# Sliding windows by DMA alone: the last staged batch shifted by one block, so that every store takes 128 partitions and the fixes are arranged anew

## The chip, the cores and the metric

One core of a Trainium2 chip. SP, ACT and POOL are engines of the core; here they compute nothing and only issue DMAs, each into a queue of its own, and 16 DMA engines carry the packets of all queues. A semaphore counts what a DMA has finished, by small "semaphore packets"; a DMA has landed when its count is full. The metric is the device time of one execution in microseconds, the median over several runs.

## The reference

```python
batch, length, dim = (32, 4096, 256)       # float32
window_size, stride = 64, 32
n_windows = (length - window_size) // stride + 1        # 127
for i in range(n_windows):
    result[:, i] = x[:, i*stride : i*stride + window_size].copy()
```

Nothing is computed. A block is 32 rows of 256 floats, 32 KB. A batch has 128 blocks. Window w of a batch is its blocks w and w+1, 64 KB, so that nearly every block is written twice. The output has 266.3 MB.

## The kernel before

There are two ways to make a batch, and the kernel mixes them.

- **Direct** (21 batches, SP's queue): a DMA copies 16 windows from DRAM to DRAM. A DMA of whole windows gives each of the 16 DMA engines two packets of 32 KB and one semaphore packet. A "split turn" makes the same copy as two DMAs of half windows: two data packets and two semaphore packets. Splitting slows this queue a little against the others; that is the purpose.
- **Staged** (11 batches, ACT's queue): the batch is loaded once, one block in each of 128 partitions, and stored twice, once as first halves and once as second halves of windows. 128 partitions make 128 half windows, but a batch has 127 windows, so each store also writes one half window of a neighbouring batch with wrong data (the "spill"). Of the direct neighbours some 15 windows are therefore left out and copied at the end, from POOL's queue, after the spilling stores have landed (the "fixes").

The last staged batch, number 30, does not spill. It is stored in four parts, and nothing waits for it but the end of the program:

```python
        if g == len(self.batches) - 1:
            for half, p0, rows in ((0, 0, 112), (0, 112, 15), (1, 1, 15), (1, 16, 112)):
                self.c.count_last(self.c.store(q, self.tiles[i], self.batches[g], half, p0, rows))
            return
        for half in (0, 1):
            self.c.store(q, self.tiles[i], self.batches[g], half).then_inc(self.stored[i], 16)
...
    staged = [*range(1, B - 3, 3), B - 2]
    direct = [b for b in range(B) if b not in staged]
...
                share += 9 if at < loads else 3
                if share >= 12:
                    share -= 12
                    turns += 4
                    c.windows(ring_d, b, first(b) + 16 * j, 16, 0)        # a split turn
                    c.windows(ring_d, b, first(b) + 16 * j, 16, 1, count=mark if todo == 3 else None)
                else:
                    turns += 3
                    c.windows(ring_d, b, first(b) + 16 * j, 16, count=mark if todo == 3 else None)
...
        ring_r.wait_ge(near, 16)          # the last direct DMA but two has landed
        for i, b in enumerate(sorted(rests, key=lambda b: max(waits[b], default=0))):
            for g in waits[b]:
                st.wait_stored(ring_r, g)
            for w, n in rest_parts(b):
                c.windows(ring_r, b, w, n, None, PIECES[i % 1], count_soft)     # 15 windows
```

Of the kernel before, what the change touches and what calls it, by code (L numbers as in the profile page):

```python
# [6 lines left out]


DIRECT, IN, OUT = 32768, 16384, 16384
PIECES = (32768,)  # L10


class Copier:


    def __init__(self, nc, tc, x, out, B, L, D, W, S, n_win):
        assert W == 2 * S and L % S == 0
        self.nc, self.tc, self.x, self.out = nc, tc, x, out
        self.B = B
        self.blk = S * D  # L20
        self.nb = L // S
        self.nw = n_win
        self.total = 0
        self.done = tc.alloc_semaphore("done")
        self.last = tc.alloc_semaphore("last")
        self.last_total = 0

    def xap(self, block, dims):
        return bass.AP(self.x.tensor, self.x.offset + block * self.blk, dims)

    def oap(self, elem, dims):
        return bass.AP(self.out.tensor, self.out.offset + elem, dims)

    def count(self, dma):
        dma.then_inc(self.done, 16)
        self.total += 16

    def count_last(self, dma):
        dma.then_inc(self.last, 16)
        self.last_total += 16  # L40

    def windows(self, q, b, w0, n, half=None, piece=DIRECT, count=None):

        blk = self.blk
        size = 2 * blk if half is None else blk
        off = blk if half else 0
        (count or self.count)(
            q.dma_start(  # L48
                out=self.oap((b * self.nw + w0) * 2 * blk + off, [[2 * blk, n], [1, size]]),
                in_=bass.AP(  # L50
                    self.x.tensor,
                    self.x.offset + (b * self.nb + w0) * blk + off,
                    [[blk, n], [1, size]],
                ),
                max_dma_last_dim=piece,
            )
        )

    def load(self, q, t, b):
        return q.dma_start(  # L60
            out=t[:, :], in_=self.xap(b * self.nb, [[self.blk, self.nb], [1, self.blk]]),
            max_dma_last_dim=IN,
        )

    def store(self, q, t, b, half, p0=0, n=None):



        blk = self.blk
        n = self.nb if n is None else n  # L70
        w = b * self.nw + p0 - half
        return q.dma_start(
            out=self.oap(w * 2 * blk + half * blk, [[2 * blk, n], [1, blk]]),
            in_=t[p0 : p0 + n, :],
            max_dma_last_dim=OUT,
        )


class Staging:


    def __init__(self, c, pool, dtype, batches, bufs):
        self.c, self.batches = c, batches
        self.tiles = [pool.tile([128, c.blk], dtype, name=f"xb{i}") for i in range(bufs)]
        self.loaded = [c.tc.alloc_semaphore(f"loaded{i}") for i in range(bufs)]
        self.stored = [c.tc.alloc_semaphore(f"stored{i}") for i in range(bufs)]

    def load(self, q, g):
        n, i = divmod(g, len(self.tiles))
        if n:  # L90
            q.wait_ge(self.stored[i], 32 * n)
        self.c.load(q, self.tiles[i], self.batches[g]).then_inc(self.loaded[i], 16)

    def store(self, q, g):
        n, i = divmod(g, len(self.tiles))
        q.wait_ge(self.loaded[i], 16 * (n + 1))
        if g == len(self.batches) - 1:

            for half, p0, rows in ((0, 0, 112), (0, 112, 15), (1, 1, 15), (1, 16, 112)):
                self.c.count_last(self.c.store(q, self.tiles[i], self.batches[g], half, p0, rows))  # L100
            return
        for half in (0, 1):
            self.c.store(q, self.tiles[i], self.batches[g], half).then_inc(self.stored[i], 16)

    def wait_stored(self, q, g):
        n, i = divmod(g, len(self.tiles))
# [12 lines left out]
@with_exitstack  # L119
def kernel(  # L120
    ctx: ExitStack,
    tc: tile.TileContext,
    x: bass.AP,
    window_size: bass.AP,
    stride: bass.AP,
    out: bass.AP,
):
    nc = tc.nc
    W, S = int(window_size), int(stride)
    B, L, D = x.shape  # L130
    n_win = (L - W) // S + 1
    assert out.shape == (B, n_win, W, D)
    c = Copier(nc, tc, x, out, B, L, D, W, S, n_win)
    staged = [*range(1, B - 3, 3), B - 2]
    direct = [b for b in range(B) if b not in staged]
    pool = ctx.enter_context(tc.tile_pool(name="xb", bufs=1))
    st = Staging(c, pool, x.dtype, staged, 6)
    ring_d, ring_s = nc.sync, nc.scalar
    spilled = staged[:-1]

    waits = {b: [g for g, n in enumerate(spilled) if abs(n - b) == 1] for b in direct}
    per, loads, stores = 6, 6 * 17, 34

    def first(b):
        return 0 if b - 1 not in spilled else 8 if len(waits[b]) == 2 else 15

    def rest_parts(b):
        if len(waits[b]) == 2:
            return [(0, 8), (120, 7)]
        return [(0 if b - 1 in spilled else 112, 15)]  # L150

    soft = tc.alloc_semaphore("soft")
    soft_total = 0

    near = tc.alloc_semaphore("near")

    def mark(dma):
        dma.then_inc(near, 16)

    def count_soft(dma):  # L160
        nonlocal soft_total
        dma.then_inc(soft, 16)
        soft_total += 16

    with tc.tile_critical():  # L165
        st.run(ring_s)

        turns = share = 0
        rests = []
        todo = 7 * len(direct)  # L170
        for b in direct:
            for j in range(7):
                at = turns % (loads + per * stores)
                share += 9 if at < loads else 3
                if share >= 12:
                    share -= 12
                    turns += 4
                    c.windows(ring_d, b, first(b) + 16 * j, 16, 0)
                    c.windows(ring_d, b, first(b) + 16 * j, 16, 1, count=mark if todo == 3 else None)
                else:  # L180
                    turns += 3
                    c.windows(ring_d, b, first(b) + 16 * j, 16, count=mark if todo == 3 else None)
                todo -= 1
            rests.append(b)

        ring_r = nc.gpsimd
        ring_r.wait_ge(near, 16)
        for i, b in enumerate(sorted(rests, key=lambda b: max(waits[b], default=0))):
            for g in waits[b]:
                st.wait_stored(ring_r, g)  # L190
            for w, n in rest_parts(b):
                c.windows(ring_r, b, w, n, None, PIECES[i % 1], count_soft)
        ring_d.wait_ge(c.done, c.total)
        ring_d.wait_ge(soft, soft_total)
        ring_d.wait_ge(c.last, c.last_total)


# [33 lines left out]
```

## Time and profile before

| what | before |
|---|---|
| time, median (three runs at first; six with those beside the changed kernel) | 752.06 us; 752.27 us |
| profiled execution | 745.32 us, span 743.5 us |
| moved by DMA | 313.16 MB at 421 GB/s |
| ACT's last store data ends (DMA records) | 732.7 us |
| POOL's last fix data ends (DMA records) | 740.1 us |

The page of the kernel before, first the DMA slices (40 equal parts of the span: busy tenths, then GB/s), then the queues (q1 is SP's, q10 ACT's, q0 POOL's: packets, MB, share of 16 engines' time):

```profile
DMA  8999999999999999999999999999999999999995
GB/s 368 431 430 427 426 436 436 423 440 420 431 432 425 427 438 420 435 427 421 439 423 408 431 434 432 434 424 433 427 437 429 430 425 437 421 435 432 414 420 191
q1 hardware_dynamic: 8080, 154.15, 48.5%
q10 hardware_dynamic: 9002, 138.35, 43.8%
q0 software_dynamic: 1008, 20.65, 6.8%
```

The engines are full from the second slice to the last but one. No engine that computes is in sight. Only the bytes, the rate and the two ends can change the time. The waits of POOL in the kernel before (us in total, times, longest):

```profile
POOL out_dram L48 <- DMA out_dram<-in_x_dram: 651.4, 1, 651.4
POOL out_dram L48 <- DMA out_dram<-xb: 22.9, 1, 22.9
```

POOL waits until SP's queue is nearly through, issues 19 fixes, waits 22.9 us for the last spilling stores and issues the other two at 685.8 us. From there to the end nothing waits for anything but bytes: two queues drain.

### The profile page before, as it was taken

The numbers are of one execution on the slowest core, as the hardware profiler recorded it, in microseconds if no ns is written. First come the engines' busy times: TensorE is split into PE (matmuls) and PEld (weight loads), VectorE is DVE, ScalarE is ACT, GpSimd is POOL, SyncE is SP. The second block draws the span as 40 slices with busy tenths as digits, with TensorE's granted clock in tenths as the row PEclk, the third lists the DMA queues.
The fourth block names the chain that finished last, engine by engine and source line by source line (L and its number), as shares of the span: only waits on it lengthen the run. The fifth ranks groups of instructions, "written<-read, shape, count | busy, mean of one in ns | idle before, by whom it ended". The sixth has DMA issues, their size and how long they took to land.

```text
span 743.5 us, 321 instructions
## 1 busy us (share of the span) xinstructions
POOL 12.4 (2%) x25
## 2 busy tenths in 40 slices
POOL 0000000000000000000000000000000000050000
DMA  8999999999999999999999999999999999999995
GB/s 368 431 430 427 426 436 436 423 440 420 431 432 425 427 438 420 435 427 421 439 423 408 431 434 432 434 424 433 427 437 429 430 425 437 421 435 432 414 420 191
DMA packets 18092, 313.16 MB, mean 421 GB/s; under 512 B 4312, under 2 KB 4312, under 8 KB 4312
## 3 DMA queue, kind: packets, MB, share of 16 engines
q1 hardware_dynamic: 8080, 154.15, 48.5%
q10 hardware_dynamic: 9002, 138.35, 43.8%
q0 software_dynamic: 1008, 20.65, 6.8%
q14 instruction: 2, 0.02, 0.0%
HBM read 220.92 MB, written 266.99 MB: 656 GB/s over the span
## 4 chain that ended last, share of the span: by engine, by line
another core or an unknown queue 91%; POOL 2%; issue 0%; POOLq 0%; SPq 0%
POOL out_dram L48 2%; POOLq L226 0%; SPq L165 0%; POOLq L107 0%
## 5 line engine op out<-in xcount | busy, mean ns | idle before, releaser
L48 POOL DMA_DIRECT2D out_dram<-in_x_dram x21 | 12.2, 584 | 674.3 <-DMA out_dram<-in_x_dram 651.4
L212 POOL MEMSET const-float32-0.0<- 128x1 f32 x1 | 0.1, 93 | 0.2 <-issue 0.2
L212 POOL MEMSET const-bfloat16-1.0<- 128x1 bf16 x1 | 0.1, 97 | 0.0
L212 POOL MEMSET const-uint8-127<- 128x1 uint8 x1 | 0.1, 93 | 0.0
L212 POOL MEMSET const-float32-1.0<- 128x1 f32 x1 | 0.1, 92 | 0.0
## 6 DMA issues: line engine op xcount, KB each, us to landing
out_dram<-in_x_dram SPq DMA_DIRECT2D x83, 1024.0 KB, 97.1
out_dram<-xb ACTq DMA_DIRECT2D x20, 4096.0 KB, 137.8
out_dram<-in_x_dram SPq DMA_DIRECT2D x128, 512.0 KB, 90.5
xb<-in_x_dram ACTq DMA_DIRECT2D x11, 4096.0 KB, 122.1
out_dram<-in_x_dram POOLq DMA_DIRECT2D x21, 960.0 KB, 46.5
out_dram<-xb ACTq DMA_DIRECT2D x2, 3584.0 KB, 127.3
out_dram<-xb ACTq DMA_DIRECT2D x2, 480.0 KB, 112.8
```

The lines of the kernel that those rows point to most:

```text
L48: q.dma_start(out=self.oap((b * self.nw + w0) * 2 * blk + off, [[2 * blk, n], [1, size]]), in_=bass.AP(self.x.tensor, self.x.offset + (b * ...
L212: nc = _bacc.Bacc("TRN2", target_bir_lowering=False, num_devices=1)
```

## The change

The last staged batch becomes number 31, and its load starts one block early: partition 0 holds the last block of batch 30, partitions 1 to 127 hold blocks 0 to 126 of batch 31. Both stores take 128 partitions (an even share for all engines), and what they spill falls into windows 125 and 126 of batch 30 alone. Those two windows are patched by a last DMA of 128 KB, after the very last store. The missing last half window of batch 31 is a DMA of 32 KB on SP's queue. Besides, the share of split turns in the store phase falls from 3/12 to 1/12.

```diff
-    staged = [*range(1, B - 3, 3), B - 2]
+    staged = [*range(1, B, 3)]
@@ load and store
-            out=t[:, :], in_=self.xap(b * self.nb, [[self.blk, self.nb], [1, self.blk]]),
+            out=t[:, :],
+            in_=self.xap(b * self.nb - shift, [[self.blk, self.nb], [1, self.blk]]),
@@ Staging.store
-        if g == len(self.batches) - 1:
-            for half, p0, rows in ((0, 0, 112), (0, 112, 15), (1, 1, 15), (1, 16, 112)):
-                self.c.count_last(...)
-            return
         for half in (0, 1):
-            self.c.store(q, self.tiles[i], self.batches[g], half).then_inc(self.stored[i], 16)
+            self.c.store(q, self.tiles[i], self.batches[g], half, self.shift(g)).then_inc(self.stored[i], 16)
@@ direct turns
-                share += 9 if at < loads else 3
+                share += 9 if turns % (loads + per * stores) < loads else 1
...
+                if todo == 7:
+                    count(c.windows(ring_d, B - 1, c.nw - 1, 1, 1, 2048), done)
@@ fixes
+            w, n = (112, 13) if b == last else (0, 15) if b - 1 in staged else (112, 15)
...
+        st.wait_stored(ring_r, len(staged) - 1)
+        ap = [[c.blk // 4, 8], [c.blk, 2], [1, c.blk // 4]]
+        oap = [[c.blk // 4, 8], [2 * c.blk, 2], [1, c.blk // 4]]
+        count(
+            ring_r.dma_start(
+                out=c.oap((last * c.nw + c.nw - 2) * 2, oap), in_=c.xap(last * c.nb + c.nw - 2, ap)
+            ),
+            rest,
+        )
```

More of the change, by code (lines that the diff above doesn't have):

```diff
@@ L9, with __init__ @@
 DIRECT, IN, OUT = 32768, 16384, 16384
-PIECES = (32768,)
 class Copier:
-    def __init__(self, nc, tc, x, out, B, L, D, W, S, n_win):
+    def __init__(self, x, out, B, L, D, W, S, n_win):
         assert W == 2 * S and L % S == 0
-        self.nc, self.tc, self.x, self.out = nc, tc, x, out
+        self.x, self.out = x, out
         self.B = B
@@ L22, in __init__ @@
         self.nw = n_win
-        self.total = 0
-        self.done = tc.alloc_semaphore("done")
-        self.last = tc.alloc_semaphore("last")
-        self.last_total = 0
     def xap(self, block, dims):
         return bass.AP(self.x.tensor, self.x.offset + block * self.blk, dims)
-    def oap(self, elem, dims):
-        return bass.AP(self.out.tensor, self.out.offset + elem, dims)
-    def count(self, dma):
-        dma.then_inc(self.done, 16)
-        self.total += 16
-    def count_last(self, dma):
-        dma.then_inc(self.last, 16)
-        self.last_total += 16
@@ L42, in windows, with oap @@
-    def windows(self, q, b, w0, n, half=None, piece=DIRECT, count=None):
-        blk = self.blk
-        size = 2 * blk if half is None else blk
-        off = blk if half else 0
-        (count or self.count)(
-            q.dma_start(
-                out=self.oap((b * self.nw + w0) * 2 * blk + off, [[2 * blk, n], [1, size]]),
-                in_=bass.AP(
-                    self.x.tensor,
-                    self.x.offset + (b * self.nb + w0) * blk + off,
-                    [[blk, n], [1, size]],
-                ),
-                max_dma_last_dim=piece,
-            )
+    def oap(self, half_window, dims):
+        return bass.AP(self.out.tensor, self.out.offset + half_window * self.blk, dims)
@@ L57, in windows, with load @@
+    def windows(self, q, b, w0, n, half=None, piece=DIRECT):
+        blk = self.blk
+        row = [1, 2 * blk if half is None else blk]
+        h = half or 0
+        return q.dma_start(
+            out=self.oap((b * self.nw + w0) * 2 + h, [[2 * blk, n], row]),
+            in_=self.xap(b * self.nb + w0 + h, [[blk, n], row]),
+            max_dma_last_dim=piece,
         )
-    def load(self, q, t, b):
+    def load(self, q, t, b, shift):
         return q.dma_start(
-            out=t[:, :], in_=self.xap(b * self.nb, [[self.blk, self.nb], [1, self.blk]]),
+            out=t[:, :],
+            in_=self.xap(b * self.nb - shift, [[self.blk, self.nb], [1, self.blk]]),
@@ L62, in load, with store @@
             max_dma_last_dim=IN,
         )
-    def store(self, q, t, b, half, p0=0, n=None):
-        blk = self.blk
-        n = self.nb if n is None else n
-        w = b * self.nw + p0 - half
+    def store(self, q, t, b, half, shift):
+        w = b * self.nw - half - shift
         return q.dma_start(
-            out=self.oap(w * 2 * blk + half * blk, [[2 * blk, n], [1, blk]]),
-            in_=t[p0 : p0 + n, :],
+            out=self.oap(2 * w + half, [[2 * self.blk, self.nb], [1, self.blk]]),
+            in_=t[:, :],
@@ L79, with __init__, shift @@
 class Staging:
-    def __init__(self, c, pool, dtype, batches, bufs):
-        self.c, self.batches = c, batches
+    def __init__(self, c, tc, pool, dtype, batches, bufs, shifted):
+        self.c, self.batches, self.shifted = c, batches, shifted
         self.tiles = [pool.tile([128, c.blk], dtype, name=f"xb{i}") for i in range(bufs)]
-        self.loaded = [c.tc.alloc_semaphore(f"loaded{i}") for i in range(bufs)]
-        self.stored = [c.tc.alloc_semaphore(f"stored{i}") for i in range(bufs)]
+        self.loaded = [tc.alloc_semaphore(f"loaded{i}") for i in range(bufs)]
+        self.stored = [tc.alloc_semaphore(f"stored{i}") for i in range(bufs)]
+    def shift(self, g):
+        return 1 if self.batches[g] in self.shifted else 0
     def load(self, q, g):
@@ L91, in load @@
             q.wait_ge(self.stored[i], 32 * n)
-        self.c.load(q, self.tiles[i], self.batches[g]).then_inc(self.loaded[i], 16)
+        self.c.load(q, self.tiles[i], self.batches[g], self.shift(g)).then_inc(self.loaded[i], 16)
     def store(self, q, g):
@@ L96, in store @@
         q.wait_ge(self.loaded[i], 16 * (n + 1))
-        if g == len(self.batches) - 1:
-            for half, p0, rows in ((0, 0, 112), (0, 112, 15), (1, 1, 15), (1, 16, 112)):
-                self.c.count_last(self.c.store(q, self.tiles[i], self.batches[g], half, p0, rows))
-            return
         for half in (0, 1):
-            self.c.store(q, self.tiles[i], self.batches[g], half).then_inc(self.stored[i], 16)
+            self.c.store(q, self.tiles[i], self.batches[g], half, self.shift(g)).then_inc(self.stored[i], 16)
     def wait_stored(self, q, g):
@@ L132, with count @@
     assert out.shape == (B, n_win, W, D)
-    c = Copier(nc, tc, x, out, B, L, D, W, S, n_win)
-    staged = [*range(1, B - 3, 3), B - 2]
+    c = Copier(x, out, B, L, D, W, S, n_win)
+    staged = [*range(1, B, 3)]
     direct = [b for b in range(B) if b not in staged]
     pool = ctx.enter_context(tc.tile_pool(name="xb", bufs=1))
-    st = Staging(c, pool, x.dtype, staged, 6)
-    ring_d, ring_s = nc.sync, nc.scalar
-    spilled = staged[:-1]
-    waits = {b: [g for g, n in enumerate(spilled) if abs(n - b) == 1] for b in direct}
-    per, loads, stores = 6, 6 * 17, 34
-    def first(b):
-        return 0 if b - 1 not in spilled else 8 if len(waits[b]) == 2 else 15
-    def rest_parts(b):
-        if len(waits[b]) == 2:
-            return [(0, 8), (120, 7)]
-        return [(0 if b - 1 in spilled else 112, 15)]
-    soft = tc.alloc_semaphore("soft")
-    soft_total = 0
-    near = tc.alloc_semaphore("near")
-    def mark(dma):
-        dma.then_inc(near, 16)
-    def count_soft(dma):
-        nonlocal soft_total
-        dma.then_inc(soft, 16)
-        soft_total += 16
+    st = Staging(c, tc, pool, x.dtype, staged, 6, {B - 1})
+    ring_d, ring_s, ring_r = nc.sync, nc.scalar, nc.gpsimd
+    done = tc.alloc_semaphore("done")
+    near = tc.alloc_semaphore("near")
+    rest = tc.alloc_semaphore("rest")
+    total = {done: 0, near: 0, rest: 0}
+    def count(dma, sem):
+        dma.then_inc(sem, 16)
+        total[sem] += 16
+    per, loads, stores = 6, 6 * 17, 34
+    todo = 7 * len(direct)
+    turns = share = 0
     with tc.tile_critical():
         st.run(ring_s)
-        turns = share = 0
-        rests = []
-        todo = 7 * len(direct)
         for b in direct:
+            w = 15 if b - 1 in staged else 0
             for j in range(7):
-                at = turns % (loads + per * stores)
-                share += 9 if at < loads else 3
+                todo -= 1
+                sem = near if todo == 2 else done
+                share += 9 if turns % (loads + per * stores) < loads else 1
                 if share >= 12:
@@ L177 @@
                     turns += 4
-                    c.windows(ring_d, b, first(b) + 16 * j, 16, 0)
-                    c.windows(ring_d, b, first(b) + 16 * j, 16, 1, count=mark if todo == 3 else None)
+                    count(c.windows(ring_d, b, w, 16, 0), done)
+                    count(c.windows(ring_d, b, w, 16, 1), sem)
                 else:
                     turns += 3
-                    c.windows(ring_d, b, first(b) + 16 * j, 16, count=mark if todo == 3 else None)
-                todo -= 1
-            rests.append(b)
-        ring_r = nc.gpsimd
+                    count(c.windows(ring_d, b, w, 16), sem)
+                w += 16
+                if todo == 7:
+                    count(c.windows(ring_d, B - 1, c.nw - 1, 1, 1, 2048), done)
         ring_r.wait_ge(near, 16)
-        for i, b in enumerate(sorted(rests, key=lambda b: max(waits[b], default=0))):
-            for g in waits[b]:
-                st.wait_stored(ring_r, g)
-            for w, n in rest_parts(b):
-                c.windows(ring_r, b, w, n, None, PIECES[i % 1], count_soft)
-        ring_d.wait_ge(c.done, c.total)
-        ring_d.wait_ge(soft, soft_total)
-        ring_d.wait_ge(c.last, c.last_total)
+        pieces = (32768,)
+        last = B - 2
+        for i, b in enumerate([*direct[:-1], last]):
+            for g, n in enumerate(staged):
+                if abs(n - b) == 1 and b != last:
+                    st.wait_stored(ring_r, g)
+            w, n = (112, 13) if b == last else (0, 15) if b - 1 in staged else (112, 15)
+            count(c.windows(ring_r, b, w, n, None, pieces[i % len(pieces)]), rest)
+        st.wait_stored(ring_r, len(staged) - 1)
[7 more added lines that the diff above has]
+        )
+        for sem in (done, near, rest):
+            ring_d.wait_ge(sem, total[sem])
 _INS = ['x', 'window_size', 'stride']
```

## The prediction

> **What bounds it now.** Not a compute engine: the program is all DMA. The page's slices show the 16 DMA engines at 90% or more from slice 2 to slice 39, 313.16 MB at a mean 421 GB/s. In the trace's DMA records a 32 KB packet takes 1.213 us (median), a 16 KB packet 0.611, a semaphore packet 0.009: packet size costs almost nothing, and 16 engines give at most about 430 GB/s; the stretches from 50 to 700 us read 419 to 439. The Trainium skill (DMA: Bandwidth & Descriptors, Where 436 GB/s comes from) puts the ceiling of the ports at 435 GB/s; this trace agrees. Only the bytes and the two ends of the span can move the time.
>
> **Bytes.** 11 staged and 21 direct batches in both kernels. The last staged batch stores 256 half windows instead of 254; POOL's fixes shrink from 315 windows to 313 plus one 128 KB patch; one 32 KB piece is new: under 0.1 MB in all, about 0.2 us. SP issues 196 DMAs instead of 211 (15 x 0.009 us, nothing). Two 15-row stores that left an engine 2.4 us less loaded (4 x 0.611) become full.
>
> **Split of the engines.** The engines seem to take turns by packet between queues. In the store phase SP's queue moves about 241 GB/s, ACT's about 187. Fewer split turns give SP 64 KB in about 3.08 turns instead of 3.25: its queue ends, and POOL's fixes start, about 8 us earlier by my turn count, and ACT's stores end that much later. The sum stays.
>
> **The tail.** Before (span clock, DMA records): ACT's stores end at 726 to 728 us on most engines, 734.0 on the slowest; POOL's fixes, which don't depend on the last stores, end at 735 to 736.5 and 740.1 on the slowest; the span ends 3.4 us after. After: the fixes and ACT's last store end about together, 735 to 736 us, slowest 739 to 740. Then comes a new serial chain: the shifted batch spills into batch 30, so the 128 KB patch may be issued only when the very last store has landed on every engine. From landing to first packet on POOL's queue took 4.8 us before (SP landing at 651.6, POOL issue of 0.6, first packet at 656.3); 8 KB packets then take about 0.6 us, their landing 0.5. That is 5 to 6 us of idle engines, all on the critical path, against at most 1 us gained by the more even last store.
>
> **Prediction.** 752.06 + 5.5 - 1 = about 756.5 us, +0.6%. Range 751 to 761. Chances: faster by over 2% 0.01, within 2% 0.95, slower by over 2% 0.04.
>
> **What would show it.** The rate between 50 and 700 us stays at 425 to 435 GB/s. SP's queue ends near 653 us instead of 661.4. POOL's wait before the fixes shortens to about 643 us; a new wait of POOL for an xb store appears at about 740 us, with one POOL DMA after it, and the chain of waits ends in it.
>
> **What would make it wrong.** If ACT's last store lands several us before POOL's fixes end, the patch hides behind them: equal, or 1 to 3 us better. If ACT's stores drag alone at the end, the loss is still the patch. If POOL's latency on an idle queue is nearer 2 us (4.8 was under load), the loss is 2 to 3 us. If HBM reads and writes clash more when SP has more of the engines, the rate falls everywhere.

## More of the kernel before

All runs told of here were at a granted clock of 1.0. The times come in two levels, whatever the kernel: in some calls the kernel before takes about 746 us, in others about 752 us. All kernels of one call run on the same chip beside the kernel before, so I compare inside a call only. The record names the chip of each call of experiments: the kernel before took 746.12 us on chip 9 and 745.34 us on chip 6, but 752.79 us on chip 15. So I take the level to go with the chip; three chips seen once each do not show that it is this and nothing else.

The profiled execution was on the faster level and the timed ones on the slower.

## The result, and the profile after

The changed kernel takes 755.61 us (755.1 to 756.9, six runs) against 752.27 us; the ratio is 1.0045, with a 95% interval of 1.0031 to 1.0059. A ratio here is the mean time of one kernel's fast runs over that of the other's in the same rounds, so not quite the ratio of the medians quoted. The change loses 0.45%: less than 2%, and clear of noise.

The page of the changed kernel, the same lines:

```profile
DMA  9999999999999999999999999999999999999994
GB/s 370 426 421 436 421 426 426 427 423 417 418 417 423 418 424 422 413 423 429 417 417 407 418 426 426 430 431 427 429 422 423 422 422 429 411 421 425 421 427 186
q1 hardware_dynamic: 7856, 154.19, 48.6%
q10 hardware_dynamic: 8976, 138.41, 43.8%
q0 software_dynamic: 1056, 20.65, 6.5%
```

The bytes agree as predicted, but the rates do not: most slices lie under those of before, and the spans differ by 10.5 us (754.0 against 743.5) where the timed runs differ by 3.3. The two profiles come from the two levels, so side by side they mislead. The waits of POOL in the changed kernel do not depend on that:

```profile
POOL out_dram L34 <- DMA out_dram<-in_x_dram: 651.5, 1, 651.5
POOL out_dram L34 <- DMA out_dram<-xb: 44.1, 1, 44.1
POOL out_dram L166 <- DMA out_dram<-xb: 39.3, 1, 39.3
```

There is a third wait, at L166, which the kernel before does not have: for the last store. The end of the chain of waits of the changed kernel (start us, us, what):

```profile
706.23 0.29 issue
706.52 1.73 POOL out_dram L34 x3
708.24 39.05 another core or an unknown queue
747.30 0.28 issue
747.58 0.56 POOL out_dram L166
```

The last store lands at 747.30; only then is the patch issued, and the program cannot end before it has landed. The page's list of DMA issues gives the patch 2.9 us from issue to landing.

### The profile page after: what moved, and what is told of

Read it like the earlier page. It is cut to its first block, busy times and chain, and to the rows that moved or that the text cites. A ratio compares the mean times of both kernels' runs of the same rounds, so it can differ in the third digit from the quotient of the medians.

```text
span 754.0 us, 305 instructions
## 1 busy us (share of the span) xinstructions
POOL 13.0 (2%) x26
## 4 chain that ended last, share of the span: by engine, by line
another core or an unknown queue 97%; POOL 2%; issue 0%; POOLq 0%; SPq 0%
POOL out_dram L34 2%; POOL out_dram L166 0%; POOLq L203 0%; SPq L131 0%; POOLq L85 0%
## 5 line engine op out<-in xcount | busy, mean ns | idle before, releaser
L166 POOL DMA_DIRECT2D out_dram<-in_x_dram x1 | 0.6, 563 | 39.3 <-DMA out_dram<-xb 39.3
```

The costliest lines, as they stand in the source:

```text
L166: ring_r.dma_start(out=c.oap((last * c.nw + c.nw - 2) * 2, oap), in_=c.xap(last * c.nb + c.nw - 2, ap)),
```

## The experiments

Two theories. **T1**: the loss is the serial patch at the end; the lower rate belongs to the chip. **T2**: the change itself lowers the rate, because SP's queue gets more of the engines. "Rate" is the data that DMA packets started between 100 and 650 us, over 550 us, from the DMA records.

| run | what it is | median us | ratio to before [95%] | rate GB/s |
|---|---|---|---|---|
| first call | before beside it: 746.12 us | | | |
| c1_before_again | before | 745.56 | 0.9988 [0.9974, 1.0002] | 427.6 |
| c2_no_patch | after, no patch (wrong) | 745.23 | 0.9993 [0.9981, 1.0006] | 426.9 |
| c3_share3 | after, old share of splits | 746.32 | 1.0012 [0.9997, 1.0026] | 428.4 |
| c4_unshift | after, last batch as before | 746.43 | 1.0001 [0.9988, 1.0013] | 426.4 |
| second call | before beside it: 752.79 us | | | |
| d1_after_again | after | 755.54 | 1.0041 [1.0023, 1.0059] | 422.4 |
| d2_patch_twice | after, patch twice | 759.13 | 1.0083 [1.0063, 1.0103] | 422.7 |
| d3_patch_act | after, patch on ACT's queue | 755.52 | 1.0038 [1.0017, 1.0059] | 422.2 |
| d4_before_share1 | before, new share of splits | 753.90 | 1.0013 [0.9992, 1.0034] | 421.4 |
| third call | before beside it: 745.34 us | | | |
| e1_before_third | before | 745.63 | 1.0000 [0.9986, 1.0014] | 428.7 |
| e2_after_third | after | 748.27 | 1.0036 [1.0022, 1.0051] | 426.7 |
| e3_row_early | patch off the tail (wrong by 32 KB) | 745.54 | 0.9999 [0.9986, 1.0013] | 426.9 |
| e4_row_early_share2 | the same, share 2 (wrong by 32 KB) | 746.01 | 1.0010 [0.9995, 1.0025] | 428.0 |

### Before and after on one chip: c1, e1, e2, d1

No edit.

> Control: the kernel before, unchanged, against itself. Ratio 1.000 within 0.002. Its second profile decides a disputed reading: in the first profiles the kernel before moved 428.5 GB/s between 100 and 400 us and the changed kernel 421.3. Theory T1 (the difference in rate is the execution's, not the change's; the loss is the serial patch at the end): this profile may read anything from 420 to 430. Theory T2 (the change lowers the rate, by giving SP's queue more of the engines in the store phase): this profile again reads 428 or more, and its span is near 743 to 745 us.

> Control: the changed kernel again, same chip as the others of this call. Ratio to before 1.003 to 1.006 as recorded. Patch alone: last store to patch landing about 3.2 us again.

> Control beside e2 on one chip. The earlier calls fell on two chips: one where the kernel before takes 746 us and moves 428 GB/s, and one where it takes 752 us and kernels of the changed kind move 422 GB/s; so the 428.9 and 422.2 GB/s of the first two profiles may be two chips. Ratio 1.000 within 0.002. If the change lowers the rate by itself, this profile's rate from 100 to 650 us lies over e2's by about 0.3% (the 1.3 GB/s between c3 and c2/c4).

> The changed kernel: 1.003 to 1.006 of before. Its last store lands after the last POOL fix, the patch about 3.2 us later. Rate from 100 to 650 us 0 to 0.4% under e1's.

c1 read a span of 744.1 us and 427.6 GB/s, but 425.8 between 100 and 400 us, the stretch that its forecast names: T1 allowed that, T2 had asked for 428 or more. Since it fell on the faster level, I take no more from it than the noise. The loss is the same on both levels: 1.0041 and 1.0036. The rates of the first two profiles (428.9 and 422.2) were mostly the two levels: beside each other, before has 428.7 and after 426.7. The rest, 0.5%, goes with the change and is taken up at c3. The tail by stretches, first the kernel before (e1), then the changed one (e2). The columns are the stretch, its length, POOL's busy time, granted clock, the DMA engines' busy share, and GB/s. A packet counts whole in the stretch in which it starts, so that a share can read a little over 1.

```profile
700.00:720.00 20.00, 0.00 (x0) 1.00 0.99 417
720.00:730.00 10.00, 0.00 (x0) 1.00 1.04 375
730.00:735.00 5.00, 0.00 (x0) 1.00 0.79 308
735.00:740.00 5.00, 0.00 (x0) 1.00 0.11 46
740.00:744.00 4.00, 0.00 (x0) 1.00 0.00 0
```

```profile
700.00:720.00 20.00, 0.83 (x2) 1.00 0.99 424
720.00:730.00 10.00, 0.00 (x0) 1.00 1.01 434
730.00:735.00 5.00, 0.00 (x0) 1.00 0.90 383
735.00:740.00 5.00, 0.02 (x1) 1.00 0.06 26
740.00:744.00 4.00, 0.54 (x1) 1.00 0.12 33
```

Up to 735 us the changed kernel is better: 434 against 375 GB/s, then 383 against 308. It catches up there what it loses in the middle (0.45% of 550 us, taken before rounding, is 2.5 us). Then comes a hole: from 735 to 744 us its engines are 6% and 12% busy. (The kernel before has a thin end too, 11% from 735 to 740 us: from 736.96 us on POOL's last three packets start one after the other, 1.21 us apart, but only the end of the program waits for them.) In the DMA records SP's data ends at 652.6 us instead of 660.1, ACT's at 739.2 instead of 733.3, POOL's fixes at 736.2 instead of 740.6. The last landing before the patch is at 739.69 us, against 741.06 for the last landing of all in the kernel before: 1.4 us gained. The patch lands at 742.73: 3.04 us given back. Together +1.7 us at the last landing. The span differs by 2.2 us, since it ends 3.5 us after the last landing in e2 and 3.0 us in e1; what makes that half microsecond, no run tells. These are single profiles; the medians of the two runs differ by 2.6 us.

### Without the patch: c2

```diff
-        st.wait_stored(ring_r, len(staged) - 1)
-        (the 128 KB patch)
+        st.wait_stored(ring_d, len(staged) - 1)
```

> The changed kernel without the last 128 KB patch and POOL's wait for it; the end of the program waits for the last store instead. Wrong result on purpose: windows 125 and 126 of batch 30 keep the garbage. T1: in the changed kernel the last store landed at 747.5 us and the patch at 750.6 (span clock), so 3.2 us come off; ratio to before 1.000 (0.998 to 1.002), about 752.3 us. T2: at most half of the loss goes, ratio 1.003 or more.

0.9993: the whole loss goes with the patch, although the rate stays at 426.9. T2 allowed at most half of it. Its output is wrong, which doesn't matter for the time.

### Without the shift: c4

```diff
-    st = Staging(c, tc, pool, x.dtype, staged, 6, {B - 1})
+    st = Staging(c, tc, pool, x.dtype, staged, 6, set())
@@ Staging.store, last batch
+            for half, p0, rows in ((0, 0, 112), (0, 112, 15), (1, 1, 15), (1, 16, 112)):
+                (a store of these rows, counted on a semaphore of its own)
@@ no patch, no 32 KB piece, 15 fix windows for batch 30
```

> The changed kernel with the last staged batch unshifted and stored in four parts (112, 15, 15, 112 rows) as the kernel before does; no patch, no 32 KB piece; the fewer split turns stay. Correct result. T1: as without the patch, ratio 1.000 (0.998 to 1.002). T2: 1.003 or more, since the direct turns are the changed kernel's.

1.0001, and correct. With the four partial stores back, and the fewer split turns kept, the loss is gone too. Partial rows against full rows (c4 against c2) make no difference that these intervals resolve. Apart from which batch comes last, c4 is also nearly the program of d4 below, on the other level.

### The patch twice: d2

```diff
+        ring_r.wait_ge(rest, total[rest])
+        count(ring_r.dma_start(out=(as the first), in_=(as the first)), rest)
```

> The changed kernel with the patch issued a second time after the first has landed: one more step of the serial chain, nothing else. T1: one step is landing to POOL issue to landing, about 3.2 us in the trace, so the ratio to before is 1.0085 to 1.0095, 3 to 3.5 us over the changed kernel. If the loss were not in the serial step (T2), the second patch should add the same anyway, so this run measures the step and does not tell the two apart.

759.13 us, 3.6 us over the changed kernel beside it by the medians and 3.2 us by the ratios, 1.0083 against 1.0041 (3 to 3.5 were expected); the ratio of 1.0083 is just under the range expected. The chain of waits of this run shows one whole step:

```profile
747.61 0.28 issue
747.89 2.82 DMA out_dram<-in_x_dram
750.71 0.28 issue
751.00 0.56 POOL out_dram L173
```

The last store lands at 747.61, the first patch at 750.71: 3.10 us a step; the second lands at 753.79, 3.08 us later. The Trainium skill (DMA: Bandwidth & Descriptors, Anatomy of one DMA) fits 2.0 us plus the bytes at 436 GB/s; for 128 KB that is an estimate of 2.3 us. The trace reads 2.8 from the patch's issue and 3.1 from the landing before it, so the trace decides.

### The patch from ACT's queue: d3

```diff
-        st.wait_stored(ring_r, len(staged) - 1)
+        st.wait_stored(ring_s, len(staged) - 1)
-            ring_r.dma_start(
+            ring_s.dma_start(
@@ the patch counts on a semaphore of its own, for which SP waits at the end
```

> The patch issued from ACT's queue instead of POOL's, with the same wait. T1: the chain stays[...]: 0.5 to 1.5 us less than the changed kernel, ratio 1.002 to 1.004. T2: no change, 1.0045.

A miss: 755.52 us against 755.54, where 0.5 to 1.5 us less were expected. The ratio, 1.0038, does lie in the range, but with 1.0041 for d1 and intervals of about 0.002 (1.5 us) the times cannot tell 0.5 us from nothing. The traces tell more. In the DMA landings the last store is at 747.30 and the patch at 750.33, 3.03 us, against 3.24 in d1 and 3.17 in the first profile of the changed kernel. The same page of the skill (Latency and other measured facts) puts the first byte of this path at about 0.6 us and of POOL's at about 1. Counted from the end of the issuing instruction to the first packet, that difference is here: 0.31 us in d3 against 0.70 to 0.74 us for POOL's patches. But ACT's instruction took 1.24 us, and POOL's took 0.56 us after a wake-up of 0.28:

```profile
747.32 1.24 ACTq L167 DMA_DIRECT2D out_dram<-in_x_dram  x1
```

So from the landing to the first packet it is 1.57 us from ACT and 1.55 to 1.58 us from POOL: ACT's longer instruction uses up what its shorter way to the first packet saves. The price lies in waiting for a landing and landing again, not in who issues.

### The old share of split turns: c3, and the new share alone: d4

```diff
# c3, in the changed kernel
-                share += 9 if turns % (loads + per * stores) < loads else 1
+                share += 9 if turns % (loads + per * stores) < loads else 3
# d4, in the kernel before
-                share += 9 if at < loads else 3
+                share += 9 if at < loads else 1
```

> The changed kernel with the old share of split turns in the store phase (3 instead of 1). T1: the sum of the bytes stays and the patch stays; but the stores now end before the POOL fixes by several us as in the kernel before, so the patch should hide in part: 1 to 4 us less than the changed kernel, ratio 0.999 to 1.003. T2: the rate comes back, ratio to before 1.000 or the patch's part of it. The profile tells: T1 wants an unchanged rate between 100 and 400 us beside the changed kernel's of these runs, and the patch issued well before the last fix landed; T2 wants a higher rate.

> The kernel before with the changed share of split turns alone (1 instead of 3 in the store phase). T1: no serial patch, the same bytes: ratio 1.000 (0.998 to 1.002). T2: the larger share of SP costs the rate: 1.003 or more, and the rate between 100 and 400 us falls below the kernel before's.

In c3 the stores end early again (732.7 us), and the patch is issued behind fixes that are still under way. The end of its chain of waits, and the patch in its list of issues (KB, us to landing):

```profile
734.21 0.28 issue
734.49 0.56 POOL out_dram L166
out_dram<-in_x_dram POOLq DMA_DIRECT2D x1, 128.0 KB, 9.4
```

The same patch is now issued at 734.5 us, 12 us before the end of the span. Its data packets are done by 738.48 us; its landing comes 9.4 us after the issue instead of 2.8, because it queues: POOL's last four fix packets start one after the other at 738.49, 739.70, 740.92 and 742.13 us, and after 738.9 us there are only three landings, at 741.25, 743.67 and 743.87 us. That looks like one engine in arrears, with the patch's last count behind its fixes; the records name no engine, and why it is behind stays open. So it is the fixes that end this profile, not the patch's data. The profiled execution is also the slowest of the five (748.71 us; the median is 746.32), so where a usual one ends is not shown. In the time the patch costs little here: 1.0012, an interval that holds 1 and reaches 1.0026. It costs where it stands alone at the end.

T2 keeps a small true part. On the faster level, the four profiles with share 1 (c2, c4, e2, e3) have rates of 426.4 to 426.9; the four profiles with share 3 on that level (the first of before, c1, e1, c3) have 427.6 to 428.9, and share 2 (e4) has 428.0. More bytes for SP's queue go with a rate lower by about 0.4%. The difference lies after 400 us: from 400 to 600 us share 1 reads 426.7 to 427.3 and share 3 429.7 to 430.3, while from 100 to 400 us the two groups overlap (426.2 to 426.7 and 425.8 to 428.5). Why, no run shows. It does not show in the time: c2, with share 1 and no patch, stands at 0.9993. d4 is inconclusive by itself: 1.0013 with an interval from 0.9992 to 1.0034 (its near twin c4 has 1.0001), and no profile of the kernel before was taken on its level.

### A repair: e3 and e4

Row 0 of the shifted tile is overwritten early with block 126 of batch 30. Then the first-half store spills nothing wrong, the second halves go first, and only what they spill has to be patched, 20 us before the end.

```diff
+        ring_r.wait_ge(st.loaded[i], 32)
+        ring_r.dma_start(out=st.tiles[i][0:1, :], in_=(block 126 of batch 30)).then_inc(st.row, 16)
         ring_r.wait_ge(near, 16)
@@ Staging.store, shifted batch
+            q.wait_ge(self.row, 16)
+            for half in (1, 0):
+                self.c.store(q, self.tiles[i], self.batches[g], half, 1).then_inc(self.end[half], 16)
@@ in place of the patch
+        ring_r.wait_ge(st.end[1], 16)
+        count(c.windows(ring_r, last, c.nw - 1, 1, 1, 2048), rest)
+        ring_d.wait_ge(st.end[0], 16)
# e4 besides: share += 9 ... else 2
```

> The changed kernel, correct, but with the patch off the tail: row 0 of the shifted tile is overwritten with block 126 of batch 30 while the earlier stores run, the second halves are stored first and the first halves last, so that only one 32 KB half window must be patched and it waits for the last store but one, which lands some 20 us before the end. T1: as without the patch, ratio to before 0.998 to 1.001, 3 us under e2. If the tail still held a serial step, it would stay at 1.003 or more.

> As e3, with 2 instead of 1 for the split turns in the store phase, halfway to the kernel before: stores and POOL fixes should end within about 2 us of each other. Ratio 0.997 to 1.001; the only version that I expect could beat both kernels, by at most 0.3%.

Both gave a wrong result, by my mistake: the old patch had also written the first half of window 125 of batch 30, which no other DMA writes, and I left it out. A block by block account of all writes finds this one 32 KB half window and no other. It is 0.01% of the bytes, so the times can be read for the mechanism, but no correct version was run; the repair (one more 32 KB DMA that waits for nothing new) is untried. The times: 0.9999 for e3, as T1 expected, with the patch issued off the tail:

```profile
700.62 19.55 another core or an unknown queue
720.17 0.28 issue
720.46 0.53 POOL out_dram L34
```

The last landing is at 739.6 us, 3.1 us before e2's. e4 shows no gain from the middle share: 1.0010, not told from 1. No version that I ran beats the kernel before.

## Why the prediction was right, point by point

- **The time** was forecast at 756.5 us and came at 755.61; the loss at 4.5 us and came at 3.3. The range, 751 to 761 us, holds the 752.06 us of the kernel before too, so the time alone tests little; the points below do.
- **The bound**: right. Bytes are equal, the engines full, and only the ends count.
- **The turns**: right. SP's data ends 7.5 us earlier on one chip (660.1 to 652.6; forecast 8; the 661.4 us of the prediction counted the last semaphore packet as well), and POOL's first wait ends at 645.1 instead of 651.7 us (forecast 643). The count of turns also gives the split between the queues. In the store phase SP moves 64 KB per 3.25 turns and ACT 256 KB per 17, a ratio of 1.31; the records from 200 to 400 us read 242.8 and 185.2 GB/s in e1, 1.31. With 3.08 turns the count gives 1.38, and e2 reads 246.6 and 179.6, 1.37. Judged from the first two profiles alone this point would have looked false, since the slower level moved everything later.
- **The serial chain at the end**: right in kind, as c2, d2 and e3 show; wrong in size. The term "That is 5 to 6 us of idle engines" measured 3.0 to 3.2 us. The part that was mis-sized is the 4.8 us between a landing and POOL's first packet, taken from the kernel before, where the engines were full of other queues' packets; on idle engines it is 1.55 us (739.69 to 741.24 in e2). The packets then took 1.14 us (0.6 was priced) and their landing 0.35 (0.5): 3.04 in all. The fix of the kernel before is also the larger DMA, but e3 shows that size is not needed: its early row is only 32 KB, goes out on POOL's queue while the engines are full (440 GB/s from 513 to 518 us), and takes 4.45 us from the landing that releases it (513.42) to its first packet (517.87). So the load is the difference. The prediction named this as what could make it wrong. One part of the step was a choice: the patch's 16 packets of 8 KB start in two waves of eight, at 741.24 to 741.45 and at 741.94 to 742.07 us, as its outer dimension of 8 suggests; whether 16 at once would be shorter was not tried.
- **"At most 1 us gained by the more even last store"**: 1.4 us at the last landing before the patch. Evener store rows are not shown to be the cause: c4 has the old rows and is level with c2 within the noise. The better rates from 720 to 735 us come from queues that end closer together.
- **"The sum stays"** was not exact: the rate in the middle fell by 0.5% and the tail gave it back. I had listed it among the risks, without a size.

## What to carry to other kernels

When the DMA engines are full from end to end, a rearrangement of the transfers wins or loses mostly at the ends (here the middle moved by 0.5% at most); look for the last transfer that waits for another one's landing, and price that step on idle engines (here 3.1 us for 128 KB), not under load. Such a step cost nothing that the intervals resolve while other transfers still drained beside it (c3, e3), and about its whole length where it stood alone (d2), so give the last work in the program no dependant, or move what it depends on forward. And compare profiles only from runs on one chip: here the level was worth twice the effect.

## What the Trainium skill lacked or had wrong

- DMA: Bandwidth & Descriptors (Queues, rings and completion order) says that an engine drains a packet of some 9 to 17 descriptors from one queue before it turns to the next. Here, if a record of the trace is one descriptor, the split between two queues fits turns of a single descriptor of 32 or 16 KB, with the semaphore packet as a turn of its own: counted 1.31 and 1.38, measured 1.31 and 1.37.
- The same page (Anatomy of one DMA) has a fixed cost of about 2.0 us. With the page's fit that is an estimate of 2.3 us for 128 KB; POOL's patches read 2.8 to 3.0 us from issue to landing on idle engines (the first profile of the changed kernel, d1, d2, e2). What a kernel pays for a DMA that waits for another's landing is more: 3.03 to 3.24 us from landing to landing (these four and d3).
- The same page (Latency and other measured facts) has a difference of 0.4 us in the first byte between the two ways of issuing. From the end of the issue to the first packet d3 agrees (0.31 us from ACT, 0.70 to 0.74 from POOL), but the passage leaves out the issue itself: 1.24 us on ACT and 0.28 and 0.56 on POOL, so that from a landing to the first packet both take about 1.6 us.
- No page has that the share of the queues changes the total rate: 426.4 to 426.9 GB/s with more for SP's queue, 427.6 to 428.9 with less, on one level between 100 and 650 us; from 100 to 400 us alone the two overlap.
- No page has that the same kernel on one core, at the same granted clock, runs at two levels: 745 to 746 us in some calls and 752 to 753 us in others.
